# Storing the two halves of x and w_in at their first use and loading them at their second

## The chip, the cores and the metric

The kernel runs on one core of one Trainium2 chip. The metric is the device time of one execution, in microseconds (us), as the median of three runs. TensorE (PE) does the matrix products, VectorE (DVE), ScalarE (ACT) and GpSimd (POOL) the work on tiles, and SyncE (SP) issues all copies between DRAM and the on-chip memory; 16 DMA engines carry them out.

## What is computed

One layer of a decoder with parallel groups of heads: 2048 rows of x, 1024 wide, all in float32.

```
proj = x @ w_in                         # 1024 x 2560, ten groups of 256 columns
q, k, v, b, c, h, p = split(proj)       # attention 8 heads x 64; conv 3 x 256; pooling 256
z = (q @ k.T) / 8, strictly causal      # stick-breaking attention:
log_a = log_sigmoid(z) + (sum of log_sigmoid(-z) over the later keys s' with s < s' < t)
attn = exp(log_a) @ v
conv = b * causal_conv3(c * h);  pool = windowed means of p, minus p, times pool_w
mix = head_rmsnorm(concat(attn, conv, pool)) @ w_o
x = layernorm(alpha * x + mix)
x = layernorm(alpha * x + relu(x @ w_up)**2 @ w_down)
```

## The kernel before

A product in float32 is made of three passes of a faster matmul type. Each operand is split into a high half (the value rounded to that type) and a low half (the value minus its high half), and each product is the sum of high times high, high times low and low times high. So before a tile of x or of a weight can be used, three things happen in `load` (L177 to L185): SP issues the copy of the raw tile from DRAM into one of four shared raw buffers (L180), ACT rounds it into the high half (L182), and DVE or POOL subtracts to get the low half (L184). Which of these two does it is decided by a count of the calls (`low_engine`, L173): two of three on DVE up to call 39, from call 40 on one of three. Every tile here is 128 partitions by 512 float32 columns, 256 KB.

x is worked on in four chunks of 512 rows, each of eight tiles; the transposed x lies in DRAM as `xt`. w_in is worked on in ten groups of 256 columns, each of four tiles ("quarters" below). Only two chunks of x (16 tiles, each as two halves) and two groups of w_in fit on the chip at a time. So the program goes over pairs of chunks:

1. `qkv((0, 1))` projects chunks 0 and 1 on the six groups 2, 0, 4, 3, 1, 5: keys of heads 0 to 3, queries of heads 0 to 3, values of heads 0 to 3, then the same for heads 4 to 7. The results go to DRAM (`kscr`, `qscr`, `vscr`), from where the attention loads them (L425, L409, L427).
2. `attention` for chunks 0 and 1 (lines L406 to L476: scores `z` L433, two sigmoids on ACT, a product scan on DVE L443/L446, a product on POOL L448, transposes L465, splitting, and the product with v L470/L471).
3. `qkv((2, 3))` and attention for chunks 2 and 3.
4. `bchp((0, 1))` and `bchp((2, 3))`: groups 9, 7, 8, 6 for convolution and pooling.
5. The output projection (`out_stage`), then the two large products of the feed-forward part (`Up`, L787 and L790, and `down`, L890 to L892).

So every chunk of x is loaded and split twice, once for `qkv` and once for `bchp`, and each of the ten groups of w_in twice, once for each pair of chunks.

The order in which an engine executes its instructions is fixed when the program is built. A scheduler places them by priority (loads and splits highest, then attention, then the dense products) and by its own forecast of when operands are there; so the dense products of one stage fill the gaps of the attention of another. At run time each engine works through its list strictly in order, and so does SP: a copy that waits holds up all copies behind it. The copies take eight completion semaphores in turn, so a copy also waits until the one eight places ahead has landed (`DMAHW0` to `DMAHW7` in the listings below).

## Time and profile before

| | |
|---|---|
| median of 3 runs | 2471.21 us (2470.14 to 2471.94) |
| the profiled execution, its own time | 2475.44 us |
| span of its trace | 2473.6 us |
| PE busy | 2406.9 us, 97% of the span |
| DVE, ACT, POOL busy | 64%, 40%, 46% |
| mean traffic of the DMA engines | 146 GB/s, 360.36 MB in all |

PE is the engine to watch: it is idle for only 3% of the span, and any time at which it has nothing to do is lost, since its work is the same in total. The other engines and the copies matter where PE waits for them. In the windows below, the columns are the stretch, its length, the busy time of each engine with the number of its instructions, the TensorE clock that was granted (1.00 is full speed), the mean busy share of the 16 DMA engines and the rate at which they moved data.

### The profile page before, as it was taken

The numbers are of one execution on the slowest core, as the hardware profiler recorded it, in microseconds if no ns is written. First come the engines' busy times: TensorE is split into PE (matmuls) and PEld (weight loads), VectorE is DVE, ScalarE is ACT, GpSimd is POOL, SyncE is SP. The second block draws the span as 40 slices with busy tenths as digits, with TensorE's granted clock in tenths as the row PEclk, the third lists the DMA queues.
The fourth block names the chain that finished last, engine by engine and source line by source line (L and its number), as shares of the span: only waits on it lengthen the run. The fifth ranks groups of instructions, "written<-read, shape, count | busy, mean of one in ns | idle before, by whom it ended". The sixth has DMA issues, their size and how long they took to land.

```text
span 2473.6 us, 33055 instructions
## 1 busy us (share of the span) xinstructions
PE 2406.9 (97%) x11728; PEld 2001.1 (81%) x11728; DVE 1589.4 (64%) x2243; ACT 991.1 (40%) x1913; POOL 1141.5 (46%) x833
## 2 busy tenths in 40 slices
PE   8999999999999999999999999999899999999997
PEld 7988888778778787777888888888688888888886
DVE  3778777888888899975666556655333333333367
ACT  4667666655765756511333222222111111111123
POOL 2558554864874856534666545554111101101137
PEclk9999999999999999999999999999999999999999
DMA  8657555622523446566665383333542212212212
GB/s 243 192 150 234 163 146 145 192 84 88 157 77 99 154 160 214 189 245 249 219 222 189 112 330 133 111 103 114 190 155 85 73 65 85 86 42 78 85 60 111
DMA packets 164853, 360.36 MB, mean 146 GB/s; under 512 B 18640, under 2 KB 35024, under 8 KB 162896
## 3 DMA queue, kind: packets, MB, share of 16 engines
q1 hardware_dynamic: 164688, 358.25, 44.9%
q8 instruction: 93, 1.52, 0.2%
q14 instruction: 72, 0.59, 0.1%
HBM read 245.19 MB, written 112.98 MB: 145 GB/s over the span
## 4 chain that ended last, share of the span: by engine, by line
PE 82%; DVE 7%; DMA 4%; POOL 3%; issue 2%; ACT 2%; SPq 0%; DVEq 0%; ACTq 0%; POOLq 0%
PE dn L890 9%; PE dn L892 9%; PE dn L891 9%; PE b L787 7%; PE c L787 5%; PE a L787 4%; PE z L433 4%; PE dn L235 4%; PE dn L236 4%; PE dn L237 4%; PE b L790 3%; PE tp L465 3%; PE c L790 2%; PE a L790 2%; PE o L471 2%
## 5 line engine op out<-in xcount | busy, mean ns | idle before, releaser
L448 POOL TENSOR_TENSOR g<-g,sig 128x512 f32<-128x512 f32 (+2 forms) x320 | 379.4, 1190 | 338.8 <-DVE g L446 146.0
L890 PE MATMUL dn<-d,ht 128*128 128x512 f32 x1024 | 399.2, 390 | 8.6 <-DVE y L894 7.6
L891 PE MATMUL dn<-d,ht 128*128 128x512 f32 x1024 | 399.1, 390 | 0.0
L892 PE MATMUL dn<-d,ht 128*128 128x512 f32 x1024 | 397.9, 390 | 0.3 <-DVE ht L867 0.3
L727 POOL TENSOR_TENSOR w<-raw,w 128x512 fp32r<-128x512 f32 x186 | 260.5, 1406 | 242.3 <-ACT w L726 238.2
L896 DVE TENSOR_TENSOR y<-dn,y 128x512 f32<-128x512 f32 x224 | 154.3, 689 | 325.0 <-PE dn L892 324.9
L853 POOL TENSOR_TENSOR d<-draw,d 128x1024 fp32r<-128x1024 f32 x32 | 76.8, 2414 | 520.1 <-ACT d L852 511.1
L446 DVE TENSOR_TENSOR_SCAN g<-beta,g,z 128x513 f32<-128x513 f32 x192 | 244.0, 1275 | 47.8 <-ACT sig L438 45.8
L866 ACT CAST ht<-draw 128x512 fp32r<-128x512 f32 x128 | 74.5, 620 | 460.5 <-PE dn L892 443.6
L436 ACT ACTIVATE beta<-z 128x512 f32<-128x512 f32 (+2 forms) x320 | 172.7, 540 | 161.2 <-PE z L433 146.8
L890 PEld LDWEIGHTS dn<-d,ht 128*128 128x128 f32 x1024 | 192.7, 188 | 49.4 <-DVE y L894 8.0
L892 PEld LDWEIGHTS dn<-d,ht 128*128 128x128 f32 x1024 | 192.6, 188 | 40.8 <-DVE ht L867 0.7
L891 PEld LDWEIGHTS dn<-d,ht 128*128 128x128 f32 x1024 | 192.8, 188 | 40.0
L726 ACT CAST w<-raw 128x512 fp32r<-128x512 f32 x186 | 114.5, 621 | 273.2 <-PE b L790 138.0
L235 PE MATMUL dn<-xh,wh 128*128 128x512 f32 x512 | 207.6, 408 | 8.1 <-ACT xh L182 4.8
L433 PE MATMUL z<-k,q 128*128 128x512 f32 (+3 forms) x640 | 193.3, 381 | 16.3 <-DVE g L446 12.2
L236 PE MATMUL dn<-xl,wh 128*128 128x512 f32 x512 | 207.2, 405 | 0.0
L237 PE MATMUL dn<-xh,wl 128*128 128x512 f32 x512 | 207.1, 405 | 0.0
L469 DVE TENSOR_TENSOR tl<-tp,th 128x512 fp32r<-128x512 f32 (+1 forms) x320 | 184.3, 596 | 31.2 <-ACT th L468 30.4
L465 PE MATMUL tp<-ident,g 128*128 128x128 f32 x1088 | 191.6, 275 | 2.0 <-POOL g L448 1.0
L787 PE MATMUL b<-x,w 128*128 128x512 f32 x768 | 189.6, 389 | 1.2 <-ACT w L726 0.9
L468 ACT CAST th<-tp 128x512 fp32r<-128x512 f32 (+1 forms) x320 | 161.5, 535 | 65.7 <-PE tp L465 53.4
(194 smaller groups left out, 4973.2 us busy)
## 6 DMA issues: line engine op xcount, KB each, us to landing
hscr<-h SPq DMA_DIRECT2D x128, 256.0 KB, 2.6
draw<-hscr SPq DMA_DIRECT2D x64, 512.0 KB, 4.0
raw<-in_w_up SPq DMA_DIRECT2D x62, 512.0 KB, 4.1
x<-tscr SPq DMA_DIRECT2D x14, 2048.0 KB, 12.0
wraw<-in_w_in SPq DMA_DIRECT2D x80, 256.0 KB, 3.3
k<-kscr SPq DMA_DIRECT2D x80, 256.0 KB, 3.1
v<-vscr SPq DMA_DIRECT2D x80, 256.0 KB, 2.9
xraw<-in_xt SPq DMA_DIRECT2D x64, 256.0 KB, 3.0
```

The costliest lines, as they stand in the source:

```text
L235: nc.tensor.matmul(ps, wh, xh, start=(d == 0), stop=False)
L236: nc.tensor.matmul(ps, wh, xl, start=False, stop=False)
L237: nc.tensor.matmul(ps, wl, xh, start=False, stop=(d == ND - 1))
L433: nc.tensor.matmul(z[:, 0:w], q[:, b, j * P:(j + 1) * P], m["k"][:, 0:w], start=(b == 0), stop=(b == 1))
L446: nc.vector.tensor_tensor_scan(left, rev, idle, st["prev"][j][:, OFF - 1:OFF], ALU.mult, ALU.bypass)
L448: nc.gpsimd.tensor_tensor(gv, gv, sig[:, 0:w], ALU.mult)
L465: nc.tensor.transpose(out=tp[:, j * P:(j + 1) * P], in_=m["g"][j][:, cols], identity=ident)
L727: self.nc.gpsimd.tensor_tensor(w[:, 1], src, w.bitcast(F)[:, 0], ALU.subtract)
L787: nc.tensor.matmul(ps, wk[:, 0, d], x[:, i, :, d, :], start=(first and d == 0 and i == 0), stop=False, skip_group_check=True)
L890: nc.tensor.matmul(ps, hh[:, ts], dh[:, ds], start=(i == 0), stop=False)
L891: nc.tensor.matmul(ps, hh[:, ts], dl[:, ds], start=False, stop=False)
L892: nc.tensor.matmul(ps, hl[:, ts], dh[:, ds], start=False, stop=(i == 3))
```

## The change

At its first use, a split tile is also written out: SP stores its high half and its low half to DRAM, into new buffers `wscr` (six groups of four quarters) and `xscr` (four chunks of eight tiles). At its second use, the raw copy, the rounding and the subtraction are left out, and SP loads the two halves straight into their buffers. This holds for all tiles of x and for groups 0 to 5 of w_in; groups 6 to 9 are loaded and split twice as before.

```diff
+    wscr = [[dram.tile([2, P, 2, 256], F, name=f"wscr{g}_{q}") for q in range(4)] for g in range(6)]
+    xscr = [[dram.tile([2, P, CH], F, name=f"xscr{c}_{d}") for d in range(ND)] for c in range(NC)]
...
-    def load(src, name, shape, bufs):
+    kept = set()
+
+    def load(src, name, shape, bufs, keep=None):
         pool = px if name == "x" else pm
+        if keep is not None and keep.tensor.name in kept:
+            h, l = (pool.tile(shape, F, name=f"{name}{n}", tag=f"{name}{n}", bufs=bufs) for n in "hl")
+            for i, t in enumerate((h, l)):
+                nc.sync.dma_start(t, keep[i])
+            return h.bitcast(R), l.bitcast(R)
         raw = pd.tile(shape, F, name=f"{name}raw", tag="raw", bufs=RAW)
         nc.sync.dma_start(raw, src)
         h = pool.tile(shape, R, name=f"{name}h", tag=f"{name}h", bufs=bufs)
         nc.scalar.copy(h, raw)
         l = pool.tile(shape, R, name=f"{name}l", tag=f"{name}l", bufs=bufs)
         low_engine().tensor_tensor(l, raw, h.bitcast(F), ALU.subtract)
+        if keep is not None:
+            kept.add(keep.tensor.name)
+            for i, t in enumerate((h, l)):
+                nc.sync.dma_start(keep[i], t.bitcast(F))
         return h, l
...
-                w.append(load(A["w_in"][g][q], "w", [P, 2, 256], ND))
+                w.append(load(A["w_in"][g][q], "w", [P, 2, 256], ND, wscr[g][q] if g < 6 else None))
...
-        return load(A["xt"][c][d], "x", [P, CH], 2 * ND)
+        return load(A["xt"][c][d], "x", [P, CH], 2 * ND, xscr[c][d])
```

In numbers: 56 second uses (24 quarters of w_in and 32 tiles of x). They lose 56 raw loads, 56 roundings on ACT, and 56 subtractions, 18 of them on DVE and 38 on POOL. SP gains 112 stores and 112 loads of 256 KB against the 56 loads that go, 168 copies more than before.

The program is scheduled anew. These are SP's first copies before. `wraw` and `xraw` are the raw tiles, the small ones are constants; what a copy waits for stands in brackets.

```order
L180 DMA wraw<-in_w_in 128x512
L180 DMA xraw<-in_xt 128x512 x2
L180 DMA wraw<-in_w_in 128x512
L149 DMA gain<-in_mix_g 128x8
L151 DMA cw<-in_conv_w 128x6
L153 DMA psc<-in_pool_scale 128x2
L180 DMA xraw<-in_xt 128x512 [waits DMAHW0_49,DVE_49]
L155 DMA rcount<-in_rcount 128x32
L180 DMA xraw<-in_xt 128x512 [waits DMAHW1_49,DVE_49]
L160 DMA pw_271<-in_pool_w 64x64 [waits DMAHW2_49]
L180 DMA wraw<-in_w_in 128x512 [waits DMAHW3_49,Pool_49]
L180 DMA xraw<-in_xt 128x512 [waits DMAHW4_49,DVE_49]
```

And these are SP's copies after, from the fourth load on (`wscr` and `xscr` are the new DRAM buffers; lines stand 2 to 13 lower in the changed file).

```order
L189 DMA wraw<-in_w_in 128x512
L151 DMA gain<-in_mix_g 128x8
L153 DMA cw<-in_conv_w 128x6
L197 DMA wscr_0_196<-wh 128x512 [waits Activation_49]
L197 DMA wscr_0_196<-wl 128x512 [waits DVE_49]
L197 DMA xscr_0_212<-xh 128x512 [waits DMAHW0_49,Activation_49]
L197 DMA xscr_0_212<-xl 128x512 [waits DMAHW1_49,DVE_49]
L197 DMA xscr_1_213<-xh 128x512 [waits DMAHW2_49,Activation_49]
L197 DMA wscr_1_197<-wh 128x512 [waits DMAHW3_49,Activation_49]
L197 DMA xscr_1_213<-xl 128x512 [waits DMAHW4_49,Pool_49]
L197 DMA wscr_1_197<-wl 128x512 [waits DMAHW5_49,DVE_49]
L189 DMA xraw<-in_xt 128x512 [waits DMAHW6_49]
```

Eight stores, each of which waits for the half it stores, now stand in SP's list ahead of the fifth load, and the pattern goes on like this through the first six groups.

The other place is where x comes in for the second time, at the start of `bchp((0, 1))`. Before, SP's list reads there as follows (`v`, `k` and `q` are loads of the attention, `vscr` stores of it):

```order
L180 DMA wraw<-in_w_in 128x512 [waits DMAHW3_49,Pool_49]
L180 DMA xraw<-in_xt 128x512 [waits DMAHW4_49,Pool_49]
L180 DMA xraw<-in_xt 128x512 [waits DMAHW5_49,Pool_49]
L258 DMA vscr_1_137<-vst 128x4x128 [waits DMAHW6_49,DVE_49]
L258 DMA vscr_1_137<-vst 128x4x128 [waits DMAHW7_49]
L180 DMA wraw<-in_w_in 128x512 [waits DMAHW3_49,DMAHW0_49,DVE_49]
L180 DMA xraw<-in_xt 128x512 [waits DMAHW1_49,Pool_49]
L427 DMA v<-vscr_0_132 128x512 [waits DMAHW2_49,PE_49]
L180 DMA xraw<-in_xt 128x512 [waits DMAHW4_49,Pool_49]
```

After, the halves come straight into the buffers of the old chunk, and each of their loads waits for PE:

```order
L440 DMA v<-vscr_0_134 128x512 [waits DMAHW0_49,PE_49]
L438 DMA k<-kscr_2_118 128x512 [waits DMAHW1_49,PE_49]
L271 DMA vscr_1_137<-vst 128x4x128 [waits DMAHW2_49,DVE_49]
L271 DMA vscr_1_137<-vst 128x4x128 [waits DMAHW3_49]
L186 DMA xh<-xscr_0_212 128x512 [waits DMAHW4_49,PE_49]
L440 DMA v<-vscr_0_132 128x512 [waits DMAHW5_49,PE_49]
L186 DMA xl<-xscr_0_212 128x512 [waits DMAHW6_49,PE_49]
L186 DMA xh<-xscr_1_213 128x512 [waits DMAHW7_49,PE_49]
L186 DMA xl<-xscr_1_213 128x512 [waits DMAHW0_49,PE_49]
```

PE's own list begins with the same 192 matmuls in both programs (keys and queries of heads 0 to 3 for both chunks). Then, before, two matmuls of the values (L250) stand ahead of the first scores `z`; after, 116 do.

## Rows read from the trace of the kernel before

**Rows 1.** The page: span, and busy time and share of the engines.
```profile
span 2473.6 us, 33055 instructions
...
PE 2406.9 (97%) x11728; PEld 2001.1 (81%) x11728; DVE 1589.4 (64%) x2243; ACT 991.1 (40%) x1913; POOL 1141.5 (46%) x833
```
**Rows 2.** Windows: stretch, length, busy by engine (count), clock, DMA share, GB/s.
```profile
core 0: us, PE busy (x) PEld busy (x) DVE busy (x) ACT busy (x) POOL busy (x), PEclk, DMA share, GB/s
0.00:60.00 60.00, 52.14 (x220) 42.15 (x221) 24.01 (x42) 25.85 (x45) 15.34 (x22) 0.97 0.84 242
60.00:120.00 60.00, 60.00 (x399) 54.98 (x398) 43.72 (x60) 37.53 (x87) 31.25 (x29) 1.00 0.70 194
120.00:180.00 60.00, 60.00 (x356) 51.92 (x354) 46.76 (x65) 40.17 (x85) 30.76 (x26) 1.00 0.54 142
180.00:240.00 60.00, 58.60 (x378) 53.14 (x377) 52.12 (x70) 43.30 (x101) 47.53 (x39) 0.97 0.83 249
240.00:300.00 60.00, 60.00 (x354) 52.13 (x353) 47.16 (x65) 40.50 (x89) 32.25 (x29) 1.00 0.60 171
420.00:480.00 60.00, 56.21 (x361) 49.43 (x359) 50.18 (x58) 44.34 (x90) 48.27 (x38) 0.99 0.70 215
600.00:660.00 60.00, 56.07 (x296) 46.14 (x294) 53.80 (x71) 39.90 (x80) 44.52 (x35) 0.97 0.47 145
1500.00:1560.00 60.00, 60.00 (x267) 49.69 (x266) 35.05 (x43) 16.73 (x30) 32.97 (x23) 1.00 0.37 123
```
**Rows 3.** The same windows over all of the later mixed stage.
```profile
420.00:1140.00 720.00, 688.55 (x3537) 560.84 (x3536) 610.43 (x884) 404.40 (x808) 444.11 (x345) 0.98 0.47 152
```
**Rows 4.** Waits of PE: line waited for, us in total, times, longest.
```profile
PE z L433 <- DVE g L446: 12.2, 13, 3.3
...
PE dn L235 <- ACT xh L182: 4.8, 1, 4.8
```
**Rows 5.** Timeline of PE at the start: start, us, instruction, idle before.
```profile
4.80 1.22 PE L235 MATMUL dn<-xh,wh 128*128 128x512 f32 x2 [4.80 <-ACT xh L182]
...
18.45 0.39 PE L237 MATMUL dn<-xh,wl 128*128 128x512 f32 x1
20.96 0.69 PE L235 MATMUL dn<-xh,wh 128*128 128x512 f32 x1 [2.12 <-DVE qk L66]
```
**Rows 6.** Line L250 (first matmul of the values): ns min/median/max, first and last start.
```profile
L250 PE MATMUL dn<-wh,xh x256: 277/282/366, 56.8 to 454.8; 128*128 128x256 f32 x128
```
**Rows 7.** Windows of 5 us while the first groups are loaded; columns as in rows 2.
```profile
20.00:25.00 5.00, 4.04 (x11) 3.17 (x12) 2.49 (x4) 2.43 (x5) 2.31 (x2) 0.66 0.93 250
25.00:30.00 5.00, 5.00 (x24) 4.10 (x23) 1.01 (x2) 1.24 (x2) 0.00 (x0) 1.00 0.94 254
30.00:35.00 5.00, 4.05 (x18) 3.08 (x17) 2.48 (x4) 2.90 (x6) 1.29 (x1) 1.00 0.93 329
35.00:40.00 5.00, 5.00 (x23) 4.10 (x22) 2.99 (x4) 1.59 (x3) 1.48 (x1) 1.00 0.88 200
```
**Rows 8.** Copies by tile: count, KB each, median us from issue to landing.
```profile
hscr<-h SPq DMA_DIRECT2D x128, 256.0 KB, 2.6
...
wraw<-in_w_in SPq DMA_DIRECT2D x80, 256.0 KB, 3.3
...
xraw<-in_xt SPq DMA_DIRECT2D x64, 256.0 KB, 3.0
```
**Rows 9.** Lines L182 and L184: durations of the splitting, ns min/median/max.
```profile
L182 ACT CAST xh<-xraw x80: 602/621/701, 4.1 to 859.1; 128x512 fp32r<-128x512 f32 x80
...
L184 POOL TENSOR_TENSOR xl<-xraw,xh x48: 1261/1298/2190, 6.1 to 860.9; 128x512 fp32r<-128x512 f32 x48
L184 DVE TENSOR_TENSOR xl<-xraw,xh x32: 657/692/1818, 4.8 to 860.2; 128x512 fp32r<-128x512 f32 x32
```
**Rows 10.** Windows of the instructions that touch raw x: DVE, ACT, POOL busy.
```profile
420.00:480.00 60.00, 3.64 (x3) 9.64 (x16) 17.88 (x13) 0.99 0.70 215
600.00:660.00 60.00, 5.29 (x7) 9.81 (x16) 12.48 (x9) 0.97 0.47 145
```
**Rows 11.** Timeline of SP: start, us, copies in a row.
```profile
20.20 1.12 SPq L271 DMA_DIRECT2D kscr<-qk  x2
...
25.29 1.02 SPq L180 DMA_DIRECT2D xraw<-in_xt  x2
```

More of the change, by code (lines that the diff above doesn't have):

```diff
@@ L120, in bcast @@
         return t
-    scr = qscr, kscr, vscr, mscr, x1scr, tscr
+    scr = qscr, kscr, vscr, mscr, x1scr, tscr, wscr, xscr
     with ExitStack() as up:
@@ L128, in phase1 @@
 def phase1(nc, tc, whole, ctx, A, ident, scr, hscr, split, rsqrt, layer_norm, bcast):
-    qscr, kscr, vscr, mscr, x1scr, tscr = scr
+    qscr, kscr, vscr, mscr, x1scr, tscr, wscr, xscr = scr
     att = ExitStack()
```

## The prediction

> **What bounds the kernel now.** I read the page first [rows 1]: PE is busy for 2406.9 of 2473.6 us, and no other engine is over 64%. So a change gains only where PE stands idle, and it costs wherever PE is made to wait. The windows of 60 us [rows 2] show where each of the two is possible. From 60 to 180 us and from 240 to 300 us PE is busy for the whole 60.00 us, so no engine that is relieved there can give anything back. From 1500 to 1560 us it is the same, with 267 matmuls of 512 columns in 60 us, 0.225 us each; that is PE's pace, and I use it below. PE's idle time lies in three places: in the first 60 us (52.14 busy), in the mixed stage from 420 to 1140 us (688.55 of 720, so 31.5 us idle [rows 3]), and in the last stages, which the change doesn't touch.
>
> The same windows, in their last two columns, show the resource that the change draws on. The DMA engines are busy for 0.84 of the first 60 us, 0.70 and 0.54 of the next two windows, and 0.83 from 180 to 240 us, where x is exchanged for the next two chunks [rows 2]. The windows of 5 us are closer still: from 20 to 40 us the share is 0.88 to 0.94 [rows 7]. So the copies are near their limit exactly where the change puts its stores. Last I read PE's waits [rows 4] and its start [rows 5]: PE waits for a loaded operand for 4.8 us at the very start and for nothing that is loaded by line 180 after that; its largest wait in the mixed stage is for the scan of the attention on DVE (12.2 us).
>
> **The splitting that goes.** 56 roundings on ACT at 0.62 us, 18 subtractions on DVE at 0.69 us and 38 on POOL at 1.30 us [rows 9] are 35, 12 and 49 us of engine time. The part of w_in (24 of the 56) falls between 180 and 420 us, where PE has next to no idle time; it gives nothing. The part of x falls into the windows from 420 to 480 and from 600 to 660 us, where the raw tiles of x keep ACT busy for 9.6 and 9.8 us, POOL for 17.9 and 12.5, DVE for 3.6 and 5.3 [rows 10]. PE is idle there for 3.8 and 3.9 us and runs at a granted clock of 0.99 and 0.97 [rows 2]; at 0.97 another 1.8 us of its 60 are lost. So the relief is worth nothing at the least and about 10 us at the most, when all of that idle time and lost clock come back. I take 6 us, since half of PE's waits there name the attention's own chain and not the splitting.
>
> **The loads that come in their place.** A half now arrives by a copy of its own that can start only when PE has finished with the old chunk. A raw load lands in 3.0 us [rows 8] but is made ahead; rounding and subtracting then take 0.62 + 1.30 = 1.9 us after the buffer is free. So each tile is ready some 1.1 us later than before, and the 16 copies of a chunk behind each other take 16 x 0.8 = 13 us (price below). What hides it is the product of the other chunk with the last group, 96 matmuls of half the width, and the attention between; without this cover each of the two exchanges would cost up to 13 us. The loads of k and v for the attention stand behind these copies in SP's list, so they wait for PE too. I leave this at zero in the sum and in the bounds of the exchange below.
>
> **The stores at the start.** This is the large term. The price of one tile of 262,144 bytes follows from rate over share. The first 60 us give 242/0.84 = 288 GB/s, 0.91 us a tile; 1500 to 1560 us, where stores of this shape run, give 123/0.37 = 332 GB/s, 0.79 us [rows 2]; the best 5 us give 329/0.93 = 354 GB/s, 0.74 us [rows 7]. The engines never ran full over 20 us, though: 0.92 on the mean from 20 to 40 us. I take 0.79/0.92 = 0.86 us, because most of what is added is full tiles of that shape. The bounds are 0.74 (best rate, no gaps) and 1.08 us (the rate really reached in the first 60 us, 242 GB/s).
>
> In SP's list after the change, the load of the last quarter of the second group (group 0, queries) is preceded by 32 stores of halves of x and 10 of halves of w_in. With the 24 raw loads (its own among them), 8 stores of keys at half size and two loads of keys it is the 72nd tile's worth of copies, where before it was the 30th. So it lands at about 0.7 + 72 x 0.86 + 3.3 = 66 us, and is split at 67.5 us [rows 8, 9]. Of the group's 96 matmuls at most 12 could be done without the three quarters that come together at the end; the other 84 take 84 x 0.225 = 18.9 us. So the values (L250) begin at about 86.4 us, where they began at 56.8 us [rows 6]: **30 us later**. With 0.74 us it is 77.8 us, 21 later; with 1.08 us 102.3 us, 45 later. Nothing covers it: PE's list has only those 192 matmuls until then, in both orders, and no attention. SP's own pace is no tighter bound: it issued two copies in 1.12 us while it waited for the eight semaphores and two in 1.02 us [rows 11], and 85 copies at 0.56 us are 48 us. Nor are the splits: POOL and ACT are busy for a quarter and under half of these 60 us [rows 2]. By the time the values run, the third group's weights (88th tile's worth, 0.7 + 88 x 0.86 + 3.3 + 2 = 82 us) are there.
>
> No stretch of [rows 2, 7] gets past 354 GB/s at full share. By the Trainium skill (DMA: Bandwidth & Descriptors, section Specifications) the fabric carries 435 GB/s; that would be an estimated 0.60 us a tile, the values at 68 us and a loss of 11 us here, and the sum would be 11 + 4 - 6 = 9 us.
>
> **The exchange of x at 180 to 300 us.** Up to 240 us the DMA engines were busy for 0.84 + 0.70 + 0.54 + 0.83 = 2.91 windows, 175 us [rows 2]. Up to the corresponding point the change adds 80 stores of the first pair and six groups, 32 stores of chunks 2 and 3 and 4 extra loads, 116 x 0.79 = 92 us. The sum, 267 us, stands against 240 + 30 = 270 us that PE needs by then. At full share it just fits, and at 0.92 it is 290 us, 20 over, of which the slack of the next window (0.60 busy) can take most. So PE loses between 0 and 13 us more here (13 being one chunk's copies uncovered); I take 4.
>
> **The sum.** 30 + 4 - 6 = 28 us more than the profiled execution's 2475.4 us, so 2503 us; this execution lies 4.2 us above the median of the runs, 2471.2 us, and on that scale the forecast is **2499 us**. Its own bounds are 21 + 0 - 10 = +11 and 45 + 13 - 0 = +58 us, 2482 to 2529 us.
>
> **The rivals.** *The freed engines win (faster).* The place is the mixed stage from 420 to 1140 us. POOL and DVE lose 30 and 9 us of work in two of its windows [rows 10], the scheduler packs the attention tighter, and most of PE's 31.5 us of idle time [rows 3] goes. For it: PE's longest wait there is for DVE, which is busy for 610 of 720 us. Against it: 9 us are little beside those 610, and the attention's scans stay as they are. With the start at its lower bound it gives 21 - 31 = -10, 2461 us. The point from which it decides is a start that loses less than what comes back, so a tile price of 0.74 us or less. Chance 0.08.
>
> *Stores hardly slow the loads (no change).* If reads and writes overlap in the copy engines, the price of a load stays, and that of a store falls well under 0.74 us. Then the start loses some 10 us and the relief gives most of them back: 10 - 7 = +3, 2474 us. For it: the hscr stores land in 2.6 us, less than a load's 3.0 to 3.3 us [rows 8]. Against it: from 35 to 40 us, when SP stored keys and loaded weights, 200 GB/s filled 0.88 of the share [rows 7], so stores of that shape are dearer, not cheaper. By the Trainium skill's 435 GB/s (the page and section named above) the time would be near this one. Chance 0.12.
>
> *SP's list becomes the bound (slower still).* Each store waits for ACT, DVE or POOL, and loads of k, q and v wait behind it, so the DMA engines have gaps and PE meets late operands through all of the first 300 us and at the two later exchanges. At 1.08 us a tile and with 13 us at the exchange of 180 to 300 us and 13 at one of the later ones it is 45 + 26 - 0 = +71, 2542 us. For it: SP's list is strictly in order and eight copies deep. Against it: the wait for a split is under 2 us each [rows 9]. Chance 0.12.
>
> *The change doesn't do what it says.* The new order has 112 stores and 112 loads of halves and 56 roundings fewer, so I give this nothing.
>
> **How the numbers follow.** The forecast has 0.68. The range of 2474 to 2529 us takes in the forecast's bounds and the middle of the second rival, and leaves out the first rival and the third. By about 0.2% (5 us) a measurement of this kernel tells a difference from none. Faster by more than that is the first rival, 0.08; within it is most of the second and the low edge of the first, 0.10; slower is the rest, 0.82.
>
> **What the new profile would show.** If the start is right, the values (L250) begin at 78 to 102 us, PE is busy for well under 45 of the first 60 us, and the DMA share there is 0.9 or more. If the exchange is right, PE is idle for a few microseconds between 200 and 340 us, with DMA shares of 0.8 and more in all windows up to 300 us. If the relief is right, PE's idle time over the 720 us that follow 450 us is some 25 us, not 31.5. The prediction is wrong if the values begin before 70 us, or if the mixed stage gives back over 15 us.

## The result, and the profile after

The changed kernel takes **2501.13 us** (median of four runs, 2498.84 to 2503.21) beside 2471.57 us of the kernel before. The ratio of the runs is 1.0113, with a 95% interval of 1.0102 to 1.0125; the two medians by themselves divide to 1.0120. It is slower by 28 to 30 us, and 2499 us had been forecast. One execution below (3361.61 us, of the kernel with x stored behind the second group) fell in a slow state with a granted clock of 0.666 and is left out. The profiled execution took 2502.17 us, 26.7 us more than the one of before (2475.44 us).

PE's busy time grows by only 5.7 us ([rows 1]: 2406.9 us before), while ACT, POOL and DVE have less to do. So of the 26.8 us by which the span grows, 21.1 us are time in which PE stands. From the page of the kernel after:

```profile
span 2500.4 us, 33123 instructions
...
PE 2412.6 (96%) x11728; PEld 1999.7 (80%) x11728; DVE 1565.4 (63%) x2225; ACT 961.5 (38%) x1857; POOL 1092.7 (44%) x795
```

The windows of after say where. The columns are those of [rows 2]; the last two are the share and the rate of the DMA engines.

```profile
0.00:60.00 60.00, 36.73 (x107) 25.79 (x108) 14.86 (x29) 17.06 (x28) 10.77 (x17) 0.83 0.94 323
60.00:120.00 60.00, 58.67 (x366) 52.70 (x365) 22.80 (x33) 21.91 (x48) 15.96 (x14) 1.00 1.02 327
120.00:180.00 60.00, 60.00 (x327) 51.31 (x326) 42.00 (x65) 36.55 (x83) 28.17 (x25) 1.00 0.81 236
180.00:240.00 60.00, 59.47 (x409) 54.19 (x408) 48.90 (x66) 42.64 (x94) 40.50 (x33) 1.00 0.90 300
240.00:300.00 60.00, 58.60 (x339) 51.01 (x338) 31.92 (x53) 28.06 (x67) 22.30 (x21) 1.00 0.95 297
420.00:480.00 60.00, 58.77 (x377) 51.85 (x376) 42.16 (x59) 33.48 (x70) 33.56 (x29) 1.00 0.89 285
600.00:660.00 60.00, 58.24 (x314) 47.67 (x312) 50.56 (x73) 35.57 (x71) 36.84 (x29) 1.00 0.68 224
1080.00:1140.00 60.00, 54.35 (x239) 43.96 (x238) 44.29 (x78) 13.21 (x23) 20.76 (x16) 0.91 0.56 205
```

In the first 60 us PE does 107 matmuls instead of 220, at a granted clock of 0.83 instead of 0.97, and the DMA engines go from 0.84 and 242 GB/s to 0.94 and 323 GB/s. The values, which began at 56.8 us [rows 6], now begin at 80.1 us:

```profile
L263 PE MATMUL dn<-wh,xh x256: 274/283/365, 80.1 to 453.0; 128*128 128x256 f32 x128
```

The waits of PE over the whole span (line waited for, us in total, times, longest) have a new first row: the rounding of x, 21.1 us, where [rows 4] had 4.8 us. The wait for the scan, 12.2 us there, is down to 6.6 us, and a wait for the norm of the last heads (`msp`) is new.

```profile
PE dn L248 <- ACT xh L191: 21.1, 5, 7.6
...
PE z L446 <- DVE g L459: 6.6, 11, 1.9
...
PE msp L313 <- ACT sqa L306: 3.3, 1, 3.3
```

PE's start as a timeline (start, length, instruction, and in brackets the idle time before it; compare [rows 5]) shows these waits one by one:

```profile
4.83 1.22 PE L248 MATMUL dn<-xh,wh 128*128 128x512 f32 x2 [4.83 <-ACT xh L191]
...
14.24 1.22 PE L248 MATMUL dn<-xh,wh 128*128 128x512 f32 x2 [3.92 <-ACT xh L191]
...
24.45 1.22 PE L248 MATMUL dn<-xh,wh 128*128 128x512 f32 x2 [4.28 <-ACT xh L191]
...
48.95 1.22 PE L248 MATMUL dn<-xh,wh 128*128 128x512 f32 x2 [7.64 <-ACT xh L191]
```

The waits up to the first values add up to 23.5 us, where they were 7.9 us before (4.8 us for x and 3.1 us for DVE). That is 15.6 of the 23.3 us by which the values are late. The other 7.7 us are pace: 46 of the first 192 matmuls follow one another at some 0.43 us instead of 0.23, where it was 22 before, and most of them stand behind these waits, at a lower granted clock. In this stretch of 5 us, right behind the wait of 4.28 us, it is 0.50, the lower of the two levels (1.2 GHz), and 12 matmuls fit in, where [rows 7] have 24 at 1.00:

```profile
25.00:30.00 5.00, 4.86 (x12) 3.32 (x11) 1.81 (x2) 1.90 (x4) 2.33 (x2) 0.50 0.90 317
```

All of the waits shown are for tiles of **x**, none for weights. The ACT engine that is named does not hold them up: it is busy for 17 of the 60 us. What is late is the copy before the rounding. SP's own timeline (start, length, copies in a row) at that place:

```profile
35.20 0.65 SPq L284 DMA_DIRECT2D kscr<-qk  x1
...
40.18 0.59 SPq L285 DMA_DIRECT2D kscr<-qk  x1
40.87 0.53 SPq L197 DMA_DIRECT2D xscr<-xh  x1
...
43.82 0.64 SPq L197 DMA_DIRECT2D xscr<-xl  x1
44.52 1.87 SPq L189 DMA_DIRECT2D xraw<-in_xt  x3
...
54.39 1.79 SPq L189 DMA_DIRECT2D wraw<-in_w_in  x3
```

The last loads of x for chunk 1 are issued at 44.52 us; before they stood at 25.29 us [rows 11]. Between 35.20 and 44.52 us SP does nothing but issue stores, eight of keys and six of halves, at 0.4 to 1.0 us each, one after another. The last loads of the second group's weights follow at 54.39 us. Up to 46 us SP's own waits add up to only 6.4 us (8.6 us up to 26 us before); some 35 of the 46 us go into the issuing itself.

Once it is issued, a raw tile of x is not much later than before. These are the loads of the first 60 us with their median time from issue to landing, before and after:

```profile
xraw<-in_xt SPq DMA_DIRECT2D x16, 256.0 KB, 2.8
xraw<-in_xt SPq DMA_DIRECT2D x16, 256.0 KB, 4.1
```

So the fuller DMA engines add 1.3 us to a load, and the 19 us lie ahead of it, in SP's list.

**The lag.** To follow the loss through the kernel I gave each matmul the time that its shape takes at full pace (0.227 us for 512 columns, about 0.12 us for 256 and 0.1 us for 128), added these up in the order of PE's list, and read from both traces when the same sum is reached. The difference is how far a kernel is behind the one before at equal work. Counting the narrow matmuls strictly by their columns instead lowers the values in the middle by 1 to 2 us and changes no step by more than 2 us. For the kernel after:

| time in before | 53 | 94 | 177 | 306 | 430 | 763 | 1073 | 1117 | end |
|---|---|---|---|---|---|---|---|---|---|
| lag, us | +23.3 | +24.5 | +24.0 | +22.6 | +23.9 | +12.4 | +19.0 | +25.0 | +26.7 |

So it loses 24 us at the start, nothing up to 430 us, wins back 11.5 us up to 763 us, and loses 14.3 us again afterwards, mainly by 1117 us.

### The profile page after: what moved, and what is told of

Its sections match the earlier page's. It is cut to its first block, busy times and chain, and to the rows that moved or that the text cites. A ratio compares the mean times of both kernels' runs of the same rounds, so it can differ in the third digit from the quotient of the medians.

```text
span 2500.4 us, 33123 instructions
## 1 busy us (share of the span) xinstructions
PE 2412.6 (96%) x11728; PEld 1999.7 (80%) x11728; DVE 1565.4 (63%) x2225; ACT 961.5 (38%) x1857; POOL 1092.7 (44%) x795
## 4 chain that ended last, share of the span: by engine, by line
PE 50%; DVE 6%; DMA 2%; issue 2%; POOL 2%; ACT 1%; SPq 0%; DVEq 0%; ACTq 0%; POOLq 0%
PE dn L903 8%; PE dn L905 8%; PE dn L904 8%; PE b L800 6%; PE c L800 4%; PE a L800 4%; PE b L803 3%; PE c L803 2%; PE a L803 2%; DVE g L459 1%; DVE tl L482 1%; POOL o L924 1%; PE dn L534 1%; PE dn L536 1%; PE dn L535 1%
## 5 line engine op out<-in xcount | busy, mean ns | idle before, releaser
L461 POOL TENSOR_TENSOR g<-g,sig 128x512 f32<-128x512 f32 (+2 forms) x320 | 387.5, 1217 | 376.0 <-DVE g L459 152.5
L248 PE MATMUL dn<-xh,wh 128*128 128x512 f32 x512 | 209.4, 413 | 25.1 <-ACT xh L191 21.1
L250 PE MATMUL dn<-xh,wl 128*128 128x512 f32 x512 | 209.1, 409 | 0.0
L446 PE MATMUL z<-k,q 128*128 128x512 f32 (+3 forms) x640 | 190.8, 379 | 14.4 <-DVE g L459 6.6
```

Source lines behind the costliest of these rows:

```text
L248: nc.tensor.matmul(ps, wh, xh, start=(d == 0), stop=False)
L250: nc.tensor.matmul(ps, wl, xh, start=False, stop=(d == ND - 1))
L446: nc.tensor.matmul(z[:, 0:w], q[:, b, j * P:(j + 1) * P], m["k"][:, 0:w], start=(b == 0), stop=(b == 1))
L461: nc.gpsimd.tensor_tensor(gv, gv, sig[:, 0:w], ALU.mult)
```

## The experiments

They are told in the order of the questions: what the start costs and why (eight kernels), then what comes later (four). The expectations call some kernels by short names: e1_stores_only is the first one here, and e3_x23 the one with only x of chunks 2 and 3.

### Only the stores

```diff
-        if keep is not None and keep.tensor.name in kept:
+        first = keep is not None and keep.tensor.name not in kept
+        if False:
...
-        if keep is not None:
+        if first:
```

> The halves are stored at the first use as in the changed kernel, but the second use loads the raw tile and splits it again; nothing is loaded back. SP's list has the same 72 tiles' worth of copies up to the second group's last weights. Theory (the stores cost at the start, the missing splits give back about 11 us in the mixed stage): the values begin at 80 us as in the changed kernel, the lag behind the kernel before is 23 us there and stays at 20 us or more through the mixed stage, total 2505 to 2515 us. Rival (what came back between 310 and 760 us has nothing to do with the splits): the same 80 us, and the total is that of the changed kernel, 2501 us, or less.

Measured: 2511.36 us, ratio 1.0154 (1.0138 to 1.0170). The values begin at 80.1 us, and the lag is +23.3 us at 53 us, as in the whole change. The start is the stores' doing alone. The two medians put the missing splits at some 10 us.

### Stores of half the size

```diff
-                nc.sync.dma_start(keep[i], t.bitcast(F))
+                cols = (slice(None), slice(0, CH // 2)) if len(shape) == 2 else (slice(None), 0)
+                nc.sync.dma_start(keep[i][cols], t.bitcast(F)[cols])
```

> As e1_stores_only, but each of the 112 stores writes only half of its columns, so the number of stores is the same and their bytes are half; what is stored is not read. Up to the second group's last weights there are 57 tiles' worth of copies instead of 72, with 46 stores instead of 42. Theory (bytes through the DMA engines): at the 0.77 us a tile that the changed kernel shows, the values begin at 24 + 57 x 0.77 = 68 us, a lag of 11 us, total 10 to 14 us below e1. Rival (SP's list: each store waits for its half and takes its place among eight semaphores): the values begin at 78 to 82 us and the total is that of e1.

Measured: 2509.01 us (1.0148; 1.0132 to 1.0164), values at 77.6 us. The DMA share in the first 60 us falls to 0.84 at 247 GB/s, no more than before the change ([rows 2]: 0.84 and 242), and yet the lag at 53 us is +20.8 us. That speaks against bytes as the cause of most of it.

### Stores of one thirty-second of the size

```diff
+                cols = (slice(None), slice(0, 16)) if len(shape) == 2 else (slice(None), 0, slice(0, 16))
+                nc.sync.dma_start(keep[i][cols], t.bitcast(F)[cols])
```

> As e1_stores_only, but each store writes only 16 of its columns or of 256, so a store carries 8 KB instead of 256 KB; what is stored is not read. The number of copies in SP's list stays, 46 stores ahead of the second group's last weights. Theory of the bytes: they are those of the kernel before and a little more, so the values begin at 57 to 60 us and the total is 2472 to 2478 us. Theory of SP's list: the values begin at 70 us or later and the total is 2490 us or more.

Measured: 2507.08 us (1.0136; 1.0121 to 1.0151). First its window of the first 60 us, then the first row of its values, then the issue of its last raw tile of x on SP:

```profile
0.00:60.00 60.00, 40.37 (x121) 29.08 (x122) 16.34 (x30) 17.46 (x28) 10.51 (x17) 0.83 0.61 156
```

```profile
L265 PE MATMUL dn<-wh,xh x256: 274/283/416, 77.0 to 457.6; 128*128 128x256 f32 x128
```

```profile
43.98 0.42 SPq L190 DMA_DIRECT2D xraw<-in_xt  x1
```

The DMA engines are now idle for 0.39 of the time, more than before the change, and the values still begin at 77.0 us. The last raw tile of x is issued at 43.98 us, about as with full stores (in the row from 44.52 us). The lag at 53 us is +20.2 us: 20 of the 23 us stay with 8 KB in place of 256 KB. So the stores' places in SP's list are enough for most of the loss; what their bytes would cost without these places is not shown by this run. By the Trainium skill (DMA: Bandwidth & Descriptors, section Issuing engines are not separate DMA queues) the time on the sequencer to initiate a copy "is usually small relative to the DMA itself". Here it is not small: SP takes 0.3 to 0.65 us for most copies whether they move 8 or 256 KB, beside some 0.8 us of the DMA engines for a copy of 256 KB (60 to 120 us of the kernel after, 327 GB/s), and the measurement decides.

### The stores on ACT's list

```diff
-                nc.sync.dma_start(keep[i], t.bitcast(F))
+                nc.scalar.dma_start(keep[i], t.bitcast(F))
```

> The changed kernel, but the 112 stores are issued by ACT and not by SP. The bytes are the same; SP's list up to the second group's last weights is that of the kernel before, 30 tiles' worth of copies without a store. Theory of the bytes: the stores go through the same 16 DMA engines at about the same time, so the values begin at 75 to 80 us. Theory of SP's list (a load waits for its place behind the stores, which wait for the splits and for the copy eight places ahead): the values begin at 57 to 66 us, a lag of 0 to 9 us, and the total is 2475 to 2490 us; ACT, which now waits for the low halves in its own list, costs some of it.

Measured: 2507.35 us (1.0138; 1.0123 to 1.0154), values at 80.1 us. This doesn't clear the bytes, because the waits moved along with the stores. ACT's waits in the first 60 us begin with these rows:

```profile
ACT xh L191 <- DMA xscr<-xl: 12.2, 3, 4.1
ACT xh L191 <- DMA xraw<-in_xt: 9.7, 3, 8.1
```

Now the roundings of x stand in ACT's list behind stores that wait, for 12.2 us in three pieces. The DMA share is 0.98 at 339 GB/s. So SP's list is one sufficient cause (the tiny stores show it); whether the bytes at full share would be a second one of nearly the same size is not told apart by this run.

### Only w_in

```diff
-        return load(A["xt"][c][d], "x", [P, CH], 2 * ND, xscr[c][d])
+        return load(A["xt"][c][d], "x", [P, CH], 2 * ND)
```

> Only the six groups of w_in are stored and loaded back, x is loaded and split twice as before. SP's list has 8 stores ahead of the second group's last weights, 38 tiles' worth of copies instead of 30. Theory: the values begin at 57 to 59 us; the splits that go fall where PE has no idle time, so nothing comes back, and the total is 2470 to 2478 us. Rival (the stores of the later groups, 14 between the second and the third, hold up the loads all the same): the lag is 8 us or more by 140 us, total 2480 us or more.

Measured: 2492.11 us (1.0076; 1.0061 to 1.0091), values at 65.8 us. Eight stores ahead of the loads cost 9 us, more than my theory allowed. And the missing splits of w_in give next to nothing back: between 430 and 763 us the lag goes from +9.8 to +5.4, some 2 us more than in the three kernels that keep all splits (2.1 to 2.8 us). The total lies where the rival put it, but the loss is there at 53 us already (a lag of +9.0), not behind the second group.

### Only x

```diff
-                w.append(load(A["w_in"][g][q], "w", [P, 2, 256], ND, wscr[g][q] if g < 6 else None))
+                w.append(load(A["w_in"][g][q], "w", [P, 2, 256], ND, None))
```

> Only x is kept (both pairs of chunks), with the stores at their first use; no half of w_in is stored, and the splits of w_in stay. It is the partner of the run that keeps w_in alone (2492 us, values from 65.8 us) and of the run that stores x behind the first values (2471 us). In SP's list 32 stores of x, nearly all ahead of the second group's weights, stand between the loads. Theory (SP's list, the loads stand behind stores that wait for their splits): the start is held up about as in the whole change, values (L263 there) from 70 to 80 us, then the relief of about 10 us: 2482 to 2492 us. Rival (it takes the stores of both to fill the list or the DMA engines, so each alone costs little): values before 63 us, 2466 to 2476 us.

Measured: 2490.39 us (1.0069; 1.0056 to 1.0083), values at 73.3 us, a lag of +16.5 us. The theory's numbers held. With w_in alone and x alone the start loses 9.0 and 16.5 us, with both 23.3.

### x stored behind the second group

```diff
+            if name == "x":
+                waiting.append((keep, h, l))
...
             proj_qk(xs, g, qscr, 0.125)
+            while waiting:
+                store(*waiting.pop(0))
             proj_v(xs, g)
```

> As the changed kernel, but the stores of x chunks 0 and 1 are given the priority of the dense work and written down after the second group, so that SP's list has 19 stores instead of 42, and 49 tiles' worth instead of 72, up to the second group's last weights; the total of copies is the same. Theory (only what stands ahead of those loads counts): the values begin at 24 + 49 x 0.77 = 62 us, a lag of 5 us, and the total is 2478 to 2487 us. Rival (the DMA engines are full to 240 us anyway, so the stores only cost later): the values begin at 62 us, but the lag grows to 20 us or more by 300 us, total 2495 us or more.

Measured: 2488.90 us (1.0060; 1.0040 to 1.0080; three executions), values at 66.4 us instead of the 62 expected, and the total is 2 us above the theory's range. The scheduler still puts 13 stores ahead of the last raw tile of x. Put side by side, the runs so far show one pattern (the count is that of SP's list):

| kernel | copies up to the 16th tile of x | stores among them | SP starts that row of loads, us | values begin, us |
|---|---|---|---|---|
| before | 36 | 0 | 25.3 | 56.8 |
| w_in only | 44 | 8 | 27.8 | 65.8 |
| x behind the second group | 49 | 13 | 28.1 | 66.4 |
| x only | 60 | 24 | 34.9 | 73.3 |
| the changed kernel | 70 | 34 | 44.5 | 80.1 |
| half stores | 74 | 38 | 44.4 | 77.6 |
| tiny stores | 74 | 38 | 44.0 | 77.0 |

From before to after it is 34 stores and 19.2 us, 0.56 us a store. The rows in the middle don't lie on that line: there the values lose more than the last tile of x does, since earlier tiles and the weights wait too.

### x stored behind the first values

Only x is kept, and four tiles at a time are stored behind each store of the values.

```diff
-            for i, t in enumerate((h, l)):
-                nc.sync.dma_start(keep[i], t.bitcast(F))
+            waiting.append((keep, h, l))
...
-                        nc.sync.dma_start(vscr[c][g][:, :, 2 * jj + j, :].rearrange("h p x -> p h x"),
-                                          vst.bitcast(F)[:, j])
+                        ld = nc.sync.dma_start(vscr[c][g][:, :, 2 * jj + j, :].rearrange("h p x -> p h x"),
+                                               vst.bitcast(F)[:, j])
+                    with tc.issue_after(ld.ins):
+                        for keep, h, l in [waiting.pop(0) for _ in range(min(4, len(waiting)))]:
+                            for i, t in enumerate((h, l)):
+                                nc.sync.dma_start(keep[i], t.bitcast(F))
```

> Only x is stored and loaded back, not w_in, and the stores of a pair of chunks are put behind the stores of the values of its first values group, four tiles at a time, out of the way of the loads at the start. Theory: the values begin at 57 us as before; the stores cost 0 to 6 us near 80 to 130 us and at the exchange of x; the missing splits of x give back about 10 us in the mixed stage. With the attention no later than before, nothing of this is given back at its end: total 2462 to 2472 us. Rival (what the mixed stage gives back is lost again before 1140 us in any case, as in e3_x23): 2472 to 2482 us.

Measured: **2470.58 us**, ratio 0.9986 (0.9976 to 0.9996), 3.6 us under before, and the values begin at 56.6 us. Its windows:

```profile
0.00:60.00 60.00, 51.43 (x221) 40.65 (x222) 23.37 (x42) 26.16 (x45) 15.36 (x22) 1.00 0.83 243
60.00:120.00 60.00, 60.00 (x388) 54.45 (x388) 39.81 (x54) 35.37 (x81) 29.65 (x27) 1.00 1.01 327
...
420.00:480.00 60.00, 60.00 (x393) 53.62 (x392) 48.01 (x67) 39.22 (x83) 36.85 (x30) 1.00 0.85 290
...
600.00:660.00 60.00, 60.00 (x332) 50.69 (x331) 47.39 (x73) 35.52 (x74) 37.61 (x30) 1.00 0.74 241
```

The same 32 stores of the first pair run at a DMA share of 1.01 while PE is busy for 60.00 of 60 us. So busy DMA engines cost PE nothing in that window. The run with x alone differs from this one only in where its stores stand, and has its values at 73.3 us and a total of 2490.39 us: what costs is that the load PE needs next stands behind the stores. And the two windows in which x comes in a second time, 56.21 and 56.07 us busy before [rows 2], are full, as the term for the relief said.

### Only x of chunks 2 and 3

```diff
+        return load(A["xt"][c][d], "x", [P, CH], 2 * ND, xscr[c][d] if c > 1 else None)
```

(and no half of w_in kept).

> Only the x tiles of chunks 2 and 3 are stored (at about 200 us) and loaded back (at about 610 us); all else is as before. Theory: no store at the start, so the values begin at 57 us; the 32 stores fall into windows with a DMA share of 0.83 and 0.60 and cost 0 to 3 us; half of the relief, 3 to 6 us, comes back. Total 2465 to 2471 us. Rival (the relief was not from the splits): 2471 to 2474 us.

Measured: 2477.68 us (1.0021; 1.0011 to 1.0031), outside what I expected. The start is untouched (values at 56.8 us), but the exchange of x at 180 to 300 us costs: the lag goes from −2.1 us at 222 to +6.6 us at 306.

```profile
180.00:240.00 60.00, 58.78 (x385) 53.23 (x384) 45.07 (x60) 37.74 (x88) 37.83 (x33) 1.00 0.98 320
240.00:300.00 60.00, 56.52 (x296) 46.88 (x296) 48.01 (x67) 41.14 (x88) 37.07 (x30) 0.91 0.75 219
```

PE does 296 matmuls in the second window, at a clock of 0.91; before it is full there at 1.00 [rows 2]. The run with x alone pays 8.5 us at the same place (+14.4 to +22.9). The whole change does not (+21.2 to +22.6), nor does the run with x behind the first values (+2.3 to +2.4), whose stores of this pair stand behind its values too. Why the whole change is spared isn't settled.

### Stores behind, and half of w_in as well

The kernel with x stored behind the first values, and in addition groups 1, 3 and 5 of w_in kept, stored at their first use:

```diff
+            if name == "x":
+                waiting.append((keep, h, l))
+            else:
+                for i, t in enumerate((h, l)):
+                    nc.sync.dma_start(keep[i], t.bitcast(F))
...
+ ... wscr[g][q] if g in (1, 3, 5) else None))
```

> x is kept and stored behind the stores of the first values, four tiles at a time, as in the run at 2471 us; in addition the halves of w_in of groups 1, 3 and 5 are kept, stored at their first use, which lies behind the second group's weights (12 of the 24 quarters, so 44 of the 56 splits of the whole change are gone; groups 0, 2 and 4, which are loaded first, are split twice as before). Theory (only what stands ahead of the first loads costs; PE is full from 180 to 420 us, so missing splits of w_in give nothing): values from 56 to 58 us, 2467 to 2474 us, no faster than the run with x alone by more than 3 us. Rival 1 (missing splits of w_in are worth as much as those of x): 2461 to 2467 us. Rival 2 (24 more stores between 60 and 180 us hold up the loads there): lag of 5 us or more by 200 us, 2475 us or more.

Measured: 2480.26 us (1.0034; 1.0022 to 1.0045), outside the theory's 2467 to 2474 us. Up to 763 us the theory held (+1.2 us at 222, −13.4 us at 763, no better than the −14.9 us with x alone). Then 18 us were lost.

### The late loss: holding back the output projection

After 763 us every changed kernel falls back, by 2 to 19 us, with and without missing splits. One part has a clear place. In the kernel after, right behind the attention's last products:

```profile
1109.16 0.95 PE L303 MATMUL msp<-blk,sqa 128*128 128x2 f32 x8
1113.44 1.11 PE L313 MATMUL msp<-ident,sqa 128*128 128x128 f32 x4 [3.33 <-ACT sqa L306]
1116.05 0.80 PE L534 MATMUL dn<-xh,mh 128*128 128x512 f32 x1 [1.49 <-ACT mh L525]
```

```profile
1110.00:1125.00 15.00, 9.35 (x26) 6.72 (x27) 10.25 (x17) 3.43 (x6) 6.79 (x5) 0.66 0.69 261
```

PE stands for the norm of the last heads with nothing to fill the time, and the granted clock of those 15 us is 0.66. The filler would be the output projection. Of its 768 matmuls, so many are used up by the time of the last scores `z`, and so much does the lag grow from 1073 to 1117 us:

| kernel | x only | x behind the values | before | x of chunks 2, 3 | half stores | w_in only | stores only | after | x behind 2nd group | behind, half of w_in | on ACT |
|---|---|---|---|---|---|---|---|---|---|---|---|
| used up | 326 | 379 | 379 | 380 | 456 | 475 | 514 | 527 | 527 | 539 | 615 |
| lag grows, us | −2.8 | −3.1 | 0 | −3.3 | −1.7 | 0.0 | +3.2 | +6.0 | +6.7 | +8.4 | +14.3 |

The kernel with tiny stores has 509 and +3.8 us. The last two runs test it: half of the loads of w_o are held back in SP's list, so that 383 of the 768 stand ahead of the last scores.

```diff
-    load_wo(EORDER[4:])
+    with tc.issue_after(vl[-13].ins):
+        load_wo(EORDER[4:])
```

(`vl` lists the attention's loads of v.) With it, the kernel with stores behind and half of w_in:

> The run that stores all of x and half of w_in behind the first loads (2480 us) lost 8.4 us on before between the last scores and the end of the output projection: at its last scores 539 of the 768 matmuls of the output projection are already used up (379 before), and PE then stands for 3.3, 1.8 and 1.5 us at the norm of the last heads. Here one thing is added: the second half of the loads of w_o is issued behind the 13th load of v from the end, so that in PE's list 383 of the 768 stand ahead of the last scores. Theory (the cover of the last norm was used up too early, and this is the late loss): no such gap, no loss there, 2468 to 2474 us. Rival (DVE is the bound from 900 to 1080 us, so PE then waits for the scans instead, 10 us more of it): 2477 to 2484 us.

Measured: 2475.06 us (1.0010; 1.0001 to 1.0019), between the two. And the changed kernel:

> The same one addition to the changed kernel itself (2501 us): the second half of the loads of w_o is issued behind the 13th load of v from the end; 383 of the 768 matmuls of the output projection then stand ahead of the last scores, instead of 527. Theory (cover used up too early): the wait for the last norm (3.3 us) goes, and the lag behind before no longer grows by 6 us between 1073 and 1117 us of before's time; 2492 to 2497 us. Rival (DVE is the bound there): PE waits for the scans instead, 2499 to 2504 us. In either case the start is untouched, values (L263) from 79 to 81 us.

Measured: 2499.79 us (1.0108; 1.0094 to 1.0121), inside the rival's range. The values begin where they did, with a lag of +23.3 us at 53 us. The gap is gone, as the theory said: the last window is full but for half a microsecond, and `msp` is no longer in the list of PE's waits.

```profile
960.00:1020.00 60.00, 55.97 (x284) 45.15 (x283) 58.47 (x85) 34.63 (x70) 39.32 (x31) 0.97 0.63 209
1020.00:1080.00 60.00, 56.78 (x283) 45.47 (x282) 56.02 (x86) 31.55 (x61) 34.69 (x27) 1.00 0.53 178
1080.00:1140.00 60.00, 59.49 (x269) 49.03 (x268) 45.59 (x83) 9.31 (x16) 19.37 (x16) 1.00 0.71 252
```

```profile
PE z L447 <- DVE g L460: 8.9, 14, 1.9
PE o L484 <- ACT th L482: 3.3, 2, 3.0
```

But most of the gain was paid earlier. Between 780 and 1140 us PE now waits 8.9 us for the scan on DVE, where the changed kernel waits 5.0 us and the one before 2.7 us, and from 763 to 1073 us the lag grows by 15.8 us instead of 6.6. Of the 9.5 us won at the gap, 2.9 us arrive at the end (+23.8 instead of +26.7); in the other kernel it is 5.4 us (−0.5 instead of +4.9). DVE is busy for 56 to 58 us in each of the windows from 960 to 1080 us above, which speaks for DVE as the limit there, wherever the filler stands; no run takes work off DVE in this stretch, so that part isn't shown. So both theories had a part. Why the order of before loses less in this stretch than every other order is open.

## Why the prediction was right, and where it was not

The total and the sign were right, with the numbers as follows; that the total came so close is luck, as the end of this section shows.

| step | forecast | measured (lag) |
|---|---|---|
| start, values later | +30 (21 to 45) | +24 (values +23.3) |
| exchange at 180 to 300 us | +4 (0 to 13) | −1 |
| from 306 to 430 us | not in the sum | +1 |
| relief by missing splits | −6 (0 to −10) | −11.5, of it 9 by the splits |
| after 763 us | not in the sum | +14 |
| sum on the profiled execution | +28 | +26.7 |

**The start.** The size lay within its bounds, and all of its signs came: values at 80.1 us (78 to 102 asked for), PE busy for 36.73 us (under 45), DMA share 0.94 (0.9 or more). The reason behind it was wrong in two places. First, the step that failed is the sentence that SP's own pace is no tighter bound. It compared SP's 48 us with the bytes' 66 us for the last quarter of the second group's weights. I worked out when those weights land and never when the last tiles of x land, which PE needs earlier. They stand behind 34 stores and wait for SP: with tiny stores, at a DMA share of 0.61, 20 of the 23 us remain, and in the kernel after a load of x lands only 1.3 us later than before once it is issued. The second group's weights come at about the same time as PE is done with chunk 1, and no wait names them. Second, the price of a tile was too high: 0.79 us over a share of 0.92. The engines did reach a share of 1.02 at 327 GB/s over 60 us, 0.80 us a tile. The best rate it names, 354 GB/s, is that of the rows it read: from 1160 to 1165 us the same trace has 433 GB/s at a share of 1.01. The two misses meet in one number, because 72 tiles at 0.80 us are 58 us, and SP comes to the loads of those weights at 54.39 us: the bytes and the list give about the same time here. Two more things stayed unseen. The sum was not tried on the kernel before: with 30 tiles it puts the values at 50 us, where they began at 56.8 [rows 6]. And it prices the matmuls behind the wait at full pace, while 7.7 of the 23.3 us are matmuls that run slower than that.

Of the rivals, "SP's list becomes the bound" had the mechanism, but as an addition to the bytes at 1.08 us a tile, with 26 us at two exchanges; that made 71 us, where the list alone cost 20. "Stores hardly slow the loads" was right on bytes (8 KB or 256 KB, 3 us apart) and wrong on the time.

**The exchange.** The lag is +24.0 us at 177 and +22.6 us at 306. The sign asked for came: shares of 0.81 or more in all windows up to 300 us, and PE idle for 1.9 us from 180 to 300 us. The cost that I feared exists, with the size I gave as its bound rather than its middle (8.7 and 8.5 us in the two runs that store chunks 2 and 3 at their first use, without w_in), but the whole change doesn't pay it.

**The relief.** It is larger than I took and about at the end of its bounds. From 430 to 763 us the lag falls by 11.5 us; in the three kernels that keep all splits it falls by 2.1 to 2.8, so the splits are worth 9 us, and the medians of the two kernels say 10 (2511 and 2501 us; their profiled executions end only 3.5 us apart, the one with the stores alone being its fastest, 2505.7 us). I had halved it because half of PE's waits there named the attention's chain. That was misread: by the trace of before the scan on DVE has 3.7 of the 3.8 us in the first window and 2.9 of the 3.9 us in the second, and no wait there names the splitting. Still the windows at 420 and 600 us fill up entirely in the run with x behind the first values, where the splits of x are gone and the start is not late, which speaks for that chain having been held up by the splits itself; no run takes away the splits alone, so this stays argued. The place was half right: x gives it and w_in next to nothing, but mostly at its second exchange: at 600 us the lag is +21.0 us, and +20.9 us in the run with the stores alone; at 763 us it is +12.4 and +19.5 us. Nor is it a fixed price for a split: from 430 to 763 us the run with only x of chunks 2 and 3, half of the tiles, wins 11.4 us, and the one with x behind the first values 18.8 us. The half loads cost nothing that shows, though a half lands in 5.2 us:

```profile
xh<-xscr SPq DMA_DIRECT2D x32, 256.0 KB, 5.2
```

**What was missing.** My sign for the relief, some 25 us of idle time in the 720 us behind 450 us, did not come:

```profile
450.00:1170.00 720.00, 682.57 (x3477) 552.18 (x3475) 613.07 (x892) 399.30 (x800) 427.02 (x332) 0.99 0.49 159
```

It is 37.4 us, against 31.5 us before in the stretch 30 us earlier [rows 3], although the relief came. The new order uses up the output projection earlier, and PE stands at the last norm: 6 of the 14 us arise at that gap, of which the run that closes it gets 2.9 us back in all. Most of the rest, 6.6 us, arises from 763 to 1073 us, where DVE is busiest; its cause is open. Without the 14 us the forecast's own terms give 24 − 1 − 11.5 = +11.5 us and 2483 us, still slower. So the number came out as near as it did because two misses, 14 us forgotten and some 16 us too much in the other terms, cancel, which is luck; the sign rests on the start and didn't need them.

## What to carry to other kernels

A copy that nobody waits for still delays those behind it in the list of the engine that issues it. Follow the load that is needed soonest, count what is put ahead of it, and use the time per issue from the trace, not the bytes alone. Try the sum on the kernel before first, and price the slower matmuls behind a wait too. Then place the stores behind the loads, where the same bytes may be free. And when a change makes a scheduler order everything anew, look at where the filler goes that covers the last dependent chain, since a gain in the middle is worth no more than what is left of it there.

## What the runs showed of the hardware

The issue of a copy takes SP about as long for 8 KB as for 256 KB: most are 0.3 to 0.65 us in the kernel after and in the one with tiny stores (the median store of 256 KB takes 0.40 to 0.51 us by kind, that of 8 KB 0.35 to 0.38 us), and with the waits in between a list of 70 to 74 copies takes 44 us.

How fast the DMA engines go differs from stage to stage. With the loads and stores of 256 KB and less at the start of the kernel after, over 5 us at full share:

```profile
30.00:35.00 5.00, 4.05 (x16) 2.94 (x15) 2.58 (x4) 2.33 (x5) 1.17 (x1) 0.88 1.05 390
50.00:55.00 5.00, 4.87 (x12) 3.73 (x12) 1.46 (x2) 1.24 (x2) 1.54 (x2) 0.50 1.03 395
```

That is 371 and 383 GB/s by rate over share; over 60 us it was 327 GB/s. The best row of [rows 7] has 329 GB/s at 0.93, so 354, but the later stages of the kernel before go higher, with copies of 512 KB and 2 MB among those of 256 KB:

```profile
1160.00:1165.00 5.00, 5.00 (x24) 4.14 (x23) 2.53 (x4) 2.29 (x4) 3.66 (x4) 1.00 1.01 433
1465.00:1470.00 5.00, 5.00 (x24) 4.14 (x23) 2.83 (x3) 1.44 (x3) 3.32 (x3) 1.00 1.05 442
```

By rate over share these are 429 and 421 GB/s. The Trainium skill (DMA: Bandwidth & Descriptors, section Specifications) states about 358 GB/s as what HBM gives one core and 435 GB/s for the fabric. All four rows lie above the first by rate over share, and the last two just below the second, so over 5 us, with one core running, the lower figure did not bind.
